# Sliding-window attention output: one bank copy, and the add of two halves moved into an accumulating DRAM transfer

## The chip, the cores and the metric

The kernel runs on one core of a Trainium2 chip. The metric is device time in microseconds, taken as the median of three runs. The profile records one execution.

The engines are named as the profile names them: PE is TensorE (its weight loads are PEld), DVE is VectorE, ACT is ScalarE, POOL is GpSimd, and SP is SyncE, which here only issues DMA transfers.

## The reference

One decoder layer over 2048 tokens with 16 meta tokens in front (model width 1024): RMSNorm, a combined input projection, two attention branches side by side (stick-breaking attention with 8 heads; sliding-window attention with 16 query heads, 2 key/value heads, a window of 128 and one sink logit per head), gates, two branch projections, a merge, an output projection, a residual and a final RMSNorm. The change lies in the sliding-window branch:

```python
def sliding_window_sink_attention(q, k, v, sinks, valid):
    ...
    scores = jnp.einsum('bnqhgd,bnkhd->bnhgqk', qb, kb) * scale      # per block of 128 queries, 256 keys
    scores = jnp.where(mask[None, :, None, None], scores, -jnp.inf)  # diff in [0, 128)
    probs = jax.nn.softmax(jnp.concatenate([scores, sink], axis=-1), axis=-1)[..., :-1]
    o = jnp.einsum('bnhgqk,bnkhd->bnqhgd', probs, vb)
    return o.reshape(B, L, Hq * d)

    y_sw = (o_sw * jax.nn.silu(sw_z)) @ w_branch_swa[l]
```

## The kernel before

Everything is float32. To keep its precision in matmuls, values are split into a high part (rounded) and a low part (the rest), and a product is made of three matmuls (high·high, high·low, low·high). Tokens are stored in reverse order, in four groups of 512 (`GT`), worked on as two halves, groups 2 and 3 first, then 0 and 1.

In each half come, in order: the projections of the sliding-window branch and part of the stick-breaking ones, the sliding-window attention (`window`), the stick-breaking attention (`stick`), and the gates. Projections run as `col_tile`: 24 matmuls of 128x512 into one of two banks `ps_g` (L412 to L414), then an evacuation by ACT and DVE. The attention is interleaved with projections by hand: `weave` takes one step of the main generator (projections) and then steps of the side generator (`attend`, later `stick`), paced by costs that each `yield` names. The order of PE's instructions is that program order. The order of the other engines' instructions, of the DMA issues on SP and of the DMAs on POOL included, is made by the framework's scheduler from its own cost model; waits are set by the framework from the data dependences.

`attend` runs 32 units per half: for each of four sets `s` of four heads (`kv = s // 2`), each of two groups `g`, and each of four blocks `i` of 128 queries. A unit passes through three steps:

- `scores`: 8 matmuls (L705) into the two banks `ps_z`, copied by ACT (L708) and masked by DVE (L709) into `sc`, whose sink column POOL fills (L698); row maximum (L711), exponentials with sums (L713), reciprocal (L714), scaling (L715).
- `turn`, three units later (`ULAG = 3`): four transposes (L739) into `ps_t`, then the split into `ph` (ACT, L114) and `pl` (DVE, L115), and four selects on POOL (L745) that build `pm`, in which the low part of one half of the keys and the high part of the other stand.
- `values`, a part of a unit later: six matmuls (L761) into the single bank `ps_o`. The left operand holds the high part of V in 64 columns and the low part in the other 64, so the bank's partitions 0 to 63 hold one partial output and 64 to 127 the other; their sum is the output of the block for four heads.

Before the change `values` copies the upper 64 partitions to a `tmp` tile (ACT, L763), and two DVE additions of 64x256 (L767) add them to the lower ones and lay the four heads out as two pairs of 128 rows in `os`, a tile with one buffer for four units. After the fourth unit two stores of 256 KB (through the helper `DMA`, L58, on SP's queue) go to the DRAM tiles `ow`.

`ow` is read again much later, by `gated`, after all the attention of its half. The tile pool of `window` is closed when its 32 units are through, and the pool of `stick` takes its memory; the first loads of `stick` are those of `kt`, `vc` and `q` (in `load_kv` and `load_q`), and its first matmul is L862. Between the last `values` and that matmul PE has gate projections.

The tile `tmp` is a ring of 9 buffers that many steps share; the weight splits on POOL are L110 and L111.

Of the kernel before, what the change touches and what calls it, by code (L numbers as in the profile page):

```python
# [7 lines left out]
F32 = mybir.dt.float32  # L8
# [3 lines left out]
ALU = mybir.AluOpType  # L12
# [4 lines left out]
P = 128  # L17
# [4 lines left out]
GT = 512  # L22
# [20 lines left out]
def f32(ap):  # L43
    return ap.bitcast(F32)
# [3 lines left out]
def tile_kernel(ctx, tc, x, xt, meta, metat, gain, w_in, w_sb, w_sw, w_out, sinks, fgain,  # L48
# [6 lines left out]
    V, A, G, T = nc.vector, nc.scalar, nc.gpsimd, nc.tensor  # L55

    def DMA(dst, src):
        nc.sync.dma_start(*(t.bitcast(F32) if t.dtype == F32R else t for t in (dst, src)))  # L58
# [6 lines left out]
    def ps(tag):  # L65
        return pp.tile([P, 512], F32, tag=tag, name="ps_" + tag, bufs={"g": 2, "z": 2, "zm": 1, "t": 2, "o": 1}[tag])
# [20 lines left out]
    def dram(name, shape, dt=F32):  # L87
        return dp.tile(shape, dt, tag=name, name=name)
# [9 lines left out]
    ow = [[dram(f"ow{p}_{g}", [P, GT]) for g in range(4)] for p in range(8)]  # L98
# [243 lines left out]
    def tmp(dt=F32, rows=P):  # L342
        return tp.tile([rows, GT], dt, tag="tmp", name="tmp", bufs=9)
# [259 lines left out]
    def window(half, groups, sp):  # L603
# [145 lines left out]
        def values(s, g, i, st):  # L749
            kv = s // 2  # L750
            blk = 4 * (g - groups[0]) + i
            if i == 0:
                os_[0] = sp.tile([P, 2, GT], F32, tag="os", name="os", bufs=1)
            o = ps("o")
            ph, pl, pm = st["p"]
            oc = o.rearrange("p (a q) -> p a q", a=4)
            for n in range(2):
                c = slice(HB * n, HB * n + HB)
                v = vv[:, blk + n, kv, :]
                for j, (lv, rp) in enumerate(((v, ph), (v, pl), (dv[kv, blk][:, n, :], pm))):  # L760
                    T.matmul(oc[:, :, c], lhsT=lv, rhs=rp[:, :, c], start=j == 0, stop=j == 2)  # L761
            t = tmp(rows=64)
            A.copy(t, o[64:128])  # L763
            ov = o[0:64].rearrange("p (b a q) -> p b a q", b=2, a=2)
            tv = t.rearrange("p (b a q) -> p b a q", b=2, a=2)
            for a in range(2):
                V.tensor_tensor(os_[0][64 * a:64 * a + 64, :, i * P:(i + 1) * P],  # L767
                                ov[:, :, a, :], tv[:, :, a, :], op=ALU.add)
            if i == 3:
                for pr in range(2):  # L770
                    DMA(ow[2 * s + pr][g], os_[0][:, pr, :])

        os_ = [None]
        ending = []

        def attend():
            units = [(s, g, i, {}) for s in range(4) for g in groups for i in range(4)]
            n = len(units)
            for u in range(n + ULAG):
                if u >= ULAG:  # L780
                    turn(*units[u - ULAG])
                yield 1.25
                if u < n:
                    last = 2 * units[u][0] + 1, units[u][1]
                    while last not in qs or (clock[0] < qs[last][1] and not ending):
                        yield 0
                    scores(*units[u])
                    if u < 4:
                        differences(0, 2 * u)
                    if u in (13, 15, 17, 19):  # L790
                        differences(1, u - 13)
                yield 0.9
                if u >= ULAG:
                    values(*units[u - ULAG])
# [150 lines left out]
    def put(hl, k, t):  # L945
        A.copy(hl[0][:, k, :], t)
        V.tensor_tensor(hl[1][:, k, :], t, f32(hl[0][:, k, :]), op=ALU.subtract)
# [307 lines left out]
    for half, groups in enumerate(halves):  # L1255
        gts = [lambda spec=spec: gate(*spec) for spec in specs[half]]
        with tc.tile_pool(name=f"swa{half}", bufs=1, side="left") as sp:
# [13 lines left out]
            q = [[lambda p=p: sw_q(p) for p in (2 * s, 2 * s + 1)] for s in range(4)]  # L1271
# [146 lines left out]
```

## Time and profile before

| | |
|---|---|
| median of three runs | 2132.24 us (2131.35 to 2132.43) |
| profiled execution: device time | 2134.33 us |
| profiled execution: span in the profile | 2132.6 us |
| granted TensorE clock | 0.999 |
| DMA | 390.93 MB, all issued from SP but for instruction fetches |

The profile's page lists busy time by engine, the span in 40 slices, the chain of work that ended last, and groups of instructions by source line, with their names as `output<-inputs`, their shapes, their count, and behind a bar the busy time in us and the mean of one in ns, then the idle time of that engine just before them and what ended it. Other views used below are: waits (who waited for whom: us in total, times, longest), busy time by stretch of time, the instructions of one tile or one line, and the order of time, where a row gives the start in us, the length in us, the engine, the line, the operation and its count; in brackets stands idle time before it and what ended it.

The two stretches in which `window` runs are 128 to 372 us and 870 to 1101 us; the first starts a little before with the last of the start-up.

### The profile page before, as it was taken

Reading aid. Unit: us, or ns where it says so; the run is one execution under the profiler, and the core shown is the slowest. Engines: PE = TensorE matmul, PEld = TensorE weight load, DVE = VectorE, ACT = ScalarE, POOL = GpSimd, SP = SyncE. Lnnn points to the kernel's source line nnn. Section 1 sums busy time; section 2 is a strip of 40 time slices with the busy share of each in tenths; the row PEclk is TensorE's granted clock in tenths of the full one; section 3 lists DMA queues with packets and bytes.
Section 4 is the critical chain, followed back from the end, with each engine's and each line's share of the span. In section 5 each row is a group of like instructions: output and inputs, shape, how many; then the busy total and the mean of one; then the engine's idle time right before and its main releaser. Section 6 shows DMA issues by size and latency. Waiting matters only on the chain.

```text
span 2132.6 us, 30750 instructions
## 1 busy us (share of the span) xinstructions
PE 2107.9 (99%) x10658; PEld 1751.0 (82%) x10658; DVE 1471.6 (69%) x2372; ACT 1078.4 (51%) x2461; POOL 268.9 (13%) x457
## 2 busy tenths in 40 slices
PE   8999999999999999999999999999999999999998
PEld 6788888888888888888888888888888888787886
DVE  7788986877877554887738888777773447454553
ACT  6677775555546335877735555555553213221121
POOL 2134343110000000232310000000000121000000
PEclk9999999999999999999999999999999999999999
DMA  9855554766448574434454334333324986568432
GB/s 336 293 186 191 177 187 170 236 193 195 147 170 321 207 256 153 160 128 175 145 178 157 122 117 139 109 118 103 116 89 170 359 288 212 177 216 308 149 94 89
DMA packets 170043, 390.93 MB, mean 183 GB/s; under 512 B 24448, under 2 KB 28288, under 8 KB 169888
## 3 DMA queue, kind: packets, MB, share of 16 engines
q1 hardware_dynamic: 169888, 388.97, 54.3%
q8 instruction: 84, 1.38, 0.3%
q14 instruction: 71, 0.58, 0.1%
HBM read 241.55 MB, written 145.18 MB: 181 GB/s over the span
## 4 chain that ended last, share of the span: by engine, by line
PE 85%; DVE 6%; ACT 3%; issue 2%; DMA 2%; POOL 0%; SPq 0%; ACTq 0%; DVEq 0%; POOLq 0%
PE ps_g L412 12%; PE ps_g L413 12%; PE ps_g L414 12%; PE ps_o L913 6%; PE ps_z L862 6%; PE ps_t L887 5%; PE ps_z L705 2%; PE ps_o L761 2%; PE ps_g L233 1%; PE ps_g L232 1%; PE ps_g L231 1%; PE ps_z L233 1%; PE ps_z L231 1%; PE ps_z L232 1%; PE ps_t L233 1%
## 5 line engine op out<-in xcount | busy, mean ns | idle before, releaser
L412 PE MATMUL ps_g<-xh,wh 128*128 128x512 f32 x1296 | 532.5, 411 | 7.6 <-ACT xh L1107 7.0
L414 PE MATMUL ps_g<-xh,wl 128*128 128x512 f32 x1296 | 509.3, 393 | 0.0
L413 PE MATMUL ps_g<-xl,wh 128*128 128x512 f32 x1296 | 509.2, 393 | 0.0
L876 DVE TENSOR_TENSOR_SCAN row<-row 128x512 f32<-128x512 f32 (+4 forms) x256 | 293.5, 1147 | 93.3 <-ACT row L866 40.4
L414 PEld LDWEIGHTS ps_g<-xh,wl 128*128 128x128 f32 x1296 | 243.8, 188 | 54.1
L412 PEld LDWEIGHTS ps_g<-xh,wh 128*128 128x128 f32 x1296 | 244.8, 189 | 47.2 <-ACT xh L1107 7.0
L866 ACT ACTIVATE row<-ps_z 128x512 f32<-128x512 f32 (+1 forms) x320 | 172.2, 538 | 212.4 <-PE ps_z L862 191.9
L413 PEld LDWEIGHTS ps_g<-xl,wh 128*128 128x128 f32 x1296 | 245.0, 189 | 38.1 <-DVE xl L1108 1.3
L114 ACT ACTIVATE wth<-ps_t 128x512 fp32r<-128x512 f32 (+1 forms) x320 | 170.7, 533 | 75.7 <-PE ps_t L887 73.8
L115 DVE SCALAR_TENSOR_TENSOR wtl<-ps_t,wth 128x512 fp32r<-128x512 f32 (+1 forms) x320 | 189.1, 591 | 25.6 <-ACT wth L114 25.1
L862 PE MATMUL ps_z<-kt,q 128*128 128x512 f32 (+3 forms) x640 | 185.5, 370 | 0.0
L887 PE MATMUL ps_t<-ident,row 128*128 128x128 f32 x1088 | 171.6, 273 | 0.1
L887 PEld LDWEIGHTS ps_t<-ident,row 128*128 128x128 f32 x1088 | 134.6, 140 | 33.7 <-DVE wtl L115 0.8
L862 PEld LDWEIGHTS ps_z<-kt,q 128*128 128x128 f32 x640 | 117.9, 188 | 23.9
L913 PE MATMUL ps_o<-wth,vc 128*128 128x512 f32 (+1 forms) x320 | 130.3, 407 | 0.8 <-ACT tmp L917 0.7
L913 PE MATMUL ps_o<-wtl,vc 128*128 128x512 f32 (+1 forms) x320 | 116.7, 365 | 0.0
L713 ACT ACTIVATE sc<-sc,nm 128x129 f32<-128x129 f32 x256 | 100.0, 393 | 27.9 <-DVE nm L711 26.6
L111 POOL TENSOR_TENSOR wl<-raw,wh 128x1024 fp32r<-128x1024 f32 (+1 forms) x28 | 59.9, 2138 | 325.8 <-ACT wh L108 297.0
L108 ACT CAST wh<-raw 128x1024 fp32r<-128x1024 f32 (+1 forms) x44 | 42.7, 971 | 89.2 <-PE ps_g L232 30.2
L874 DVE TENSOR_TENSOR_SCAN row<-row,mask 128x512 f32<-128x512 f32 (+2 forms) x64 | 67.9, 1066 | 19.9 <-ACT row L866 11.5
L567 ACT ACTIVATE tmp<-ps_g 128x512 f32<-128x512 f32 x84 | 50.2, 597 | 61.4 <-PE ps_g L414 49.9
L871 POOL TENSOR_SCALAR_AFFINE_SELECT row<-row 128x128 f32<-128x128 f32 x64 | 20.2, 315 | 469.5 <-ACT row L866 469.5
(435 smaller groups left out, 4092.0 us busy)
## 6 DMA issues: line engine op xcount, KB each, us to landing
wh<-h_in_w_in SPq DMA_DIRECT2D x66, 512.0 KB, 3.7
wl<-l_in_w_in SPq DMA_DIRECT2D x66, 512.0 KB, 4.6
raw<-in_w_in SPq DMA_DIRECT2D x50, 512.0 KB, 5.4
h_in_w_in<-wh SPq DMA_DIRECT2D x50, 512.0 KB, 3.4
l_in_w_in<-wl SPq DMA_DIRECT2D x50, 512.0 KB, 3.8
q<-qd SPq DMA_DIRECT2D x128, 128.0 KB, 3.2
vc<-vd SPq DMA_DIRECT2D x48, 256.0 KB, 2.9
kd<-tmp SPq DMA_DIRECT2D x32, 256.0 KB, 4.6
```

The costliest lines, as they stand in the source:

```text
L114: A.activation(h, acc, AF.Copy, scale=scale)
L115: V.scalar_tensor_tensor(l, acc, scale, f32(h), op0=ALU.mult, op1=ALU.subtract)
L412: T.matmul(acc, lhsT=wh[:, k, :], rhs=xh[g][:, k, :], start=k == 0, stop=False)
L413: T.matmul(acc, lhsT=wh[:, k, :], rhs=xl[g][:, k, :], start=False, stop=False)
L414: T.matmul(acc, lhsT=wl[:, k, :], rhs=xh[g][:, k, :], start=False, stop=k == KT - 1)
L713: A.activation(sc[:, hh, :], sc[:, hh, :], AF.Exp, bias=nm[:, hh:hh + 1], accum_out=den[:, hh:hh + 1])
L862: T.matmul(z[:, :w], lhsT=lq, rhs=kt[h][:, k0:k0 + w], start=t == 0, stop=t == 1)
L866: A.activation(r[:, :w], z[:, :w], AF.Sigmoid, scale=-1.0)
L874: V.tensor_tensor_scan(r[:, :w], r[:, :w], mask[:, :w], 1.0, op0=ALU.mult, op1=ALU.max)
L876: V.tensor_tensor_scan(r[:, :w], r[:, :w], r[:, :w], last[j] if n else 1.0, op0=ALU.mult, op1=ALU.min)
L887: T.transpose(tr[:, j * P:(j + 1) * P], rows_of[h, g, n - (j > i), j][:, k0:k0 + P], ident)
L913: T.matmul(o[:, :n], lhsT=v, rhs=r, start=first and r is wh, stop=last)
```

## The change

ACT copies the whole bank `ps_o` (both partial outputs, 128x512) into `os`, which now holds two units (128 partitions, four heads, 256 queries) with the same size and still one buffer. The `tmp` tile and the two DVE additions are gone. After every second unit the lower 64 partitions go by two plain stores to `ow`, and then the upper 64 partitions by two transfers issued from POOL with `accum_op=ALU.add`, which add to what stands in DRAM. Each of the four transfers moves 128 KB: 64 partitions, two heads, 256 queries. In place of 32 stores of 256 KB there are 64 plain ones and 64 accumulating ones. The accumulating transfers depend on the plain ones, since they read and write the same bytes.

```diff
         def values(s, g, i, st):
             kv = s // 2
             blk = 4 * (g - groups[0]) + i
-            if i == 0:
-                os_[0] = sp.tile([P, 2, GT], F32, tag="os", name="os", bufs=1)
+            if i % 2 == 0:
+                os_[0] = sp.tile([P, 4, 2 * P], F32, tag="os", name="os", bufs=1)
             o = ps("o")
...
-            t = tmp(rows=64)
-            A.copy(t, o[64:128])
-            ov = o[0:64].rearrange("p (b a q) -> p b a q", b=2, a=2)
-            tv = t.rearrange("p (b a q) -> p b a q", b=2, a=2)
-            for a in range(2):
-                V.tensor_tensor(os_[0][64 * a:64 * a + 64, :, i * P:(i + 1) * P],
-                                ov[:, :, a, :], tv[:, :, a, :], op=ALU.add)
-            if i == 3:
-                for pr in range(2):
-                    DMA(ow[2 * s + pr][g], os_[0][:, pr, :])
+            A.copy(os_[0][:, :, i % 2 * P:(i % 2 + 1) * P], oc)
+            if i % 2:
+                for n, put in ((0, DMA), (1, lambda o, i: G.dma_start(out=o, in_=i, accum_op=ALU.add))):
+                    for pr in range(2):
+                        put(ow[2 * s + pr][g][:, (i - 1) * P:(i + 1) * P].rearrange("(a d) t -> d a t", a=2),
+                            os_[0][64 * n:64 * n + 64, 2 * pr:2 * pr + 2, :])
```

## The prediction

> **What bounds the kernel now.** I read the page first, then busy time by stretch, TensorE's waits, the groups by line, and at last the order of time around the edited lines.
>
> ```profile
> span 2132.6 us, 30750 instructions
> PE 2107.9 (99%) x10658; PEld 1751.0 (82%) x10658; DVE 1471.6 (69%) x2372; ACT 1078.4 (51%) x2461; POOL 268.9 (13%) x457
> ```
>
> TensorE (PE) is busy nearly everywhere. An edit can win only the time in which PE stands idle near it, and loses all of what it makes PE wait. The edited function runs in two stretches, 128 to 372 us and 870 to 1101 us. This is the sum row of busy time over 128 to 250, 250 to 372, 870 to 985 and 985 to 1101 us, and below it PE's waits in the whole program that fall there:
>
> ```profile
> sum 475.00, PE 469.28 PEld 404.03 DVE 366.65 ACT 335.69 POOL 167.07; mean PE 117.32 PEld 101.01 DVE 91.66 ACT 83.92 POOL 41.77
> ```
>
> ```profile
> PE ps_zm L525 <- DVE tmp L115: 2.2, 2, 1.4
> PE ps_o L761 <- DVE os L767: 1.8, 2, 1.5
> PE ps_z L705 <- DVE sc L709: 1.2, 2, 0.7
> PE ps_o L761 <- POOL pm L745: 0.8, 2, 0.6
> ```
>
> (Columns: us in total, times, longest.) PE is idle for 475.00 − 469.28 = 5.7 us there: the whole prize. VectorE (DVE) ends most of it, the adds that the change removes (L767) 1.8 us.
>
> **What is removed.** The adds and their neighbours, from the groups by line:
>
> ```profile
> L767 DVE TENSOR_TENSOR os<-ps_o,tmp 64x256 f32<-64x256 f32 x128 | 52.9, 413 | 7.0 <-ACT tmp L763 5.7
> L917 ACT COPY tmp<-ps_o 128x512 f32<-128x512 f32 x32 | 18.8, 586 | 19.5 <-PE ps_o L913 18.4 <-DMA q<-qd 0.7
> L110 POOL TENSOR_SCALAR wh<-raw 128x1024 fp32r<-128x1024 f32 x21 | 25.5, 1215 | 75.0 <-DMA h_in_w_in<-wh 28.0 <-PE ps_t L423 18.2 <-PE ps_g L413 13.4
> L111 POOL TENSOR_TENSOR wl<-raw,wh 128x1024 fp32r<-128x1024 f32 (+1 forms) x28 | 59.9, 2138 | 325.8 <-ACT wh L108 297.0 <-DMA q<-qd 17.8 <-DMA raw<-in_w_sw 7.6
> ```
>
> 128 adds of 413 ns leave DVE: 52.9 us. Nearly all of it ran beside PE's matmuls, so only PE's idle time can come back: 0 to 5.7 us. I take 2.5: the 1.8 that waits on the adds by name, and a little of the 3.4 that waits on other DVE work. The bank `ps_o` also comes free about 0.8 us earlier, after the copy alone; the next unit's matmuls need it a whole unit later, so that is worth nothing more.
>
> **The copy.** ScalarE (ACT) copies the whole bank instead of half. In time by line:
>
> ```profile
> L763 ACT COPY tmp<-ps_o x32: 567/583/587, 129.6 to 366.5; 64x512 f32<-64x512 f32 x32
> L763 ACT COPY tmp<-ps_o x32: 569/583/586, 870.5 to 1098.0; 64x512 f32<-64x512 f32 x32
> ```
>
> The half-bank copy has a median of 583 ns, and the full-bank copy of L917 takes 586: 64 times 3 ns, nothing. The rows also give the rhythm: 31 gaps in 236.9 us is 7.64 us a unit in the first stretch, and 31 in 227.5 is 7.34 in the second.
>
> **The transfers.** Before, one pair of 256 KB stores for four units. After, for each two units two plain 128 KB stores on SyncE's queue (SP) and two accumulating ones on GpSimd's (POOL): 64 and 64.
>
> ```profile
> ow<-os SPq DMA_DIRECT2D x32, 256.0 KB, 2.3
> od<-tmp SPq DMA_DIRECT2D x64, 128.0 KB, 2.4
> tmp<-ow SPq DMA_DIRECT2D x16, 256.0 KB, 5.2
> L58 SPq DMA_DIRECT2D ow<-os x32: 319/403/772, 157.1 to 1099.9; - x32
> ```
>
> (The first three: KB each, median us to landing.) SP gets 32 more issues of 0.403 us, 13 us over 475, in which it mostly waits for inputs anyway: nothing. The halved transfer lands no sooner: 128 KB from 64 partitions (`od`) 2.4 us, 256 KB from 128 partitions 2.3. The Trainium skill, page "DMA: Bandwidth & Descriptors", section "Rules for kernel authors", says that two transfers to disjoint partition halves gain nothing over one of 128 partitions, and speaks against the new cut; the two rows agree.
>
> Now a chain exists that did not before. The accumulating store reads and rewrites what the plain one wrote, so POOL waits until that one has landed, and `os` (one buffer, now refilled every two units instead of four) comes free only when both accumulating stores have landed. From the start of the odd unit's copy: copy 0.59, first plain store landed 2.3 later, at 2.9. Two POOL issues: the trace has no DMA from POOL, so an issue costs between SP's 0.4 and POOL's longest common instruction (L111, 2.14); I take 1.2, as L110, a plain POOL instruction. That is 5.3. Landing: at least a store's 2.3, at most a read-back and a store one after the other, 5.2 + 2.3 = 7.5; I take 3.0, nearer the store, since one transfer does both. **Round trip 8.3 us**, bounds 2.9 + 0.8 + 2.3 = 6.0 and 2.9 + 4.3 + 7.5 = 14.7. The Trainium skill, same page, section "Anatomy of one DMA", fits a POOL-issued DMA with 2.0 us plus bytes over 436 GB/s, an estimate of 2.3 us here; by that alone the round trip would be 7.6 and the sum about 6 us instead of 11. No run shows such a transfer yet.
>
> **Who waits.** Three queues get a new wait at their head.
>
> ACT: the next even unit's copy waits for `os`; behind it stand `ph` (the first step to the next values), the exponentials and the evacuations of `ps_g`. The round trip exceeds the mean gap of 7.64 or 7.34 us by 0.7 to 1.0 us, 30 times: 25 us of later copies. ACT has 475.00 − 335.69 = 139 us idle, 4.4 a pair, and PE feels it only where the path copy, `ph`, `pl`, `pm`, values has no cover. Two units of that path, one tight and one loose:
>
> ```profile
> 257.68 0.58 ACT L763 COPY tmp<-ps_o 64x512 f32<-64x512 f32 x1
> 260.58 1.80 POOL L745 TENSOR_SCALAR_AFFINE_SELECT pm<-pl 64x256 fp32r<-64x256 f32 x2 [0.73 <-DVE pl L115]
> 262.48 0.28 PE L761 MATMUL ps_o<-pm,xs 128*128 128x256 f32 x1
> ...
> 241.16 0.58 ACT L763 COPY tmp<-ps_o 64x512 f32<-64x512 f32 x1
> 243.44 0.89 POOL L745 TENSOR_SCALAR_AFFINE_SELECT pm<-pl 64x256 fp32r<-64x256 f32 x2 [0.81 <-DVE pl L115]
> 247.06 0.28 PE L761 MATMUL ps_o<-pm,xs 128*128 128x256 f32 x1
> ```
>
> In the first the select ends at 262.38 and its matmul starts at 262.48: cover 0.1 us. In the second it is 2.7. I take one sixth of the 25 us: **+4**, bounds 0 and 25.
>
> POOL: while it waits for the plain store and then issues for 2.4 us, the selects of `pm`, the sink columns of `sc` and some weight copies (L110, L111) stand behind. By the rows above, the second pair of selects starts 2.28 and 2.90 us after a copy starts, and the plain store lands at 2.9. Mostly the selects are just ahead; where they are not, they start 2.4 us late against cover of 0.1 to 2.7, about 1 us for PE. I take five pairs of 32: **+5**, bounds 0 and 32 × 2.3 = 74.
>
> SP: a later copy makes its store later, with weight loads behind it; ACT's row covers that already.
>
> The handover to the next stage is the third place. Its tiles take this pool's memory, and the first K loads wait for the last `ow` store. Waits of SP's queue at the two handovers, and both in order of time:
>
> ```profile
> SPq L58 <- DMA ow<-os: 1.9, 1, 1.9
> SPq L58 <- DMA ow<-os: 4.0, 1, 4.0
> ```
>
> ```profile
> 366.50 0.58 ACT L763 COPY tmp<-ps_o 64x512 f32<-64x512 f32 x1 [2.15 <-PE ps_o L761]
> 367.99 0.80 SPq L58 DMA_DIRECT2D ow<-os  x2
> 370.82 0.50 SPq L58 DMA_DIRECT2D kt<-kd  x1
> 374.68 2.37 SPq L58 DMA_DIRECT2D q<-qd  x4
> 381.28 0.39 PE L862 MATMUL ps_z<-kt,q 128*128 128x512 f32 x1
> ...
> 1098.01 0.58 ACT L763 COPY tmp<-ps_o 64x512 f32<-64x512 f32 x1
> 1099.50 0.86 SPq L58 DMA_DIRECT2D ow<-os  x2
> 1104.55 1.12 SPq L58 DMA_DIRECT2D kt<-kd  x2
> 1112.45 1.89 SPq L58 DMA_DIRECT2D q<-qd  x3
> 1120.30 0.63 PE L862 MATMUL ps_z<-kt,q 128*128 128x512 f32 x2
> ```
>
> ```profile
> DMA to landing us min/median/max: 2.7/3.9/4.7
> DMA to landing us min/median/max: 3.7/3.8/4.4
> ```
>
> (The last two: `q` loads at each handover.) First handover: copy ends 367.1, plain store landed 369.4, two issues 371.8, landed 374.8, against K loads at 370.82: 4.0 us later. The last `q` load that PE needs was issued about 376.5 and landed 3.9 later at 380.4; PE wanted it at 381.28: cover 0.9, so PE stands 3.1. Second: 1098.6, landed after issue and the 4.0 of that place about 1103.0, 1105.4, 1108.4, against 1104.55: 3.9 later; `q` came at 1113.7 + 3.8 = 1117.5 for 1120.30, cover 2.8, PE stands 1.1. Together **+4.2**, bounds 0.8 (issue 0.4, landing 2.3) and 17 (2.14, 7.5).
>
> **Sum.** −2.5 + 4 + 5 + 4.2 = +10.7 us. The profiled execution took 2134.33 us, 1.7 more than its span and 2.1 more than the median of 2132.24; it would take 2145, and the median goes to **2143 us**. A measurement of this kernel can tell about 0.2%, 4.3 us, from no change; the forecast is slower by 0.5%.
>
> **Rivals.** *DVE was the brake* (0.13). DVE is busy 366.65 of 475 us, and three of the four waits quoted end at DVE or at POOL behind it. If the round trip stays below the gaps, about 7 us, and POOL's issues fall behind the selects, all 5.7 us of idle time can go and the handovers cost 0.8: −4.9, 2127.3. Against it: it needs landing near a plain store's, and issues near SP's 0.4.
>
> *A wash* (0.22). Round trip between 6 and 8 us, so that ACT's copy waits a little where ACT would idle, POOL costs nothing, the handovers 2 to 4: −2.5 + 3 = about 0, 2133. For it: 139 us of idle ACT, and DVE's relief shortens `pl`, which feeds the selects.
>
> *The accumulating write is slow* (0.17). It fetches its destination from DRAM before it writes; at the bound of 7.5 us the round trip is 2.9 + 2.4 + 7.5 = 12.8. That passes the mean gap of 7.5 by 5.3 and ACT's idle time of 4.4 a pair by 0.9: 32 × 0.9 = 29 for PE, handovers 7.6 + 5.5 = 13, POOL 5, less 2.5: +45, 2177. It decides once the round trip passes about 12 us.
>
> That the add doesn't take place I exclude: the low half is in the output only by this transfer.
>
> **How the numbers follow.** The forecast (+4.3 to +30 us) has 0.48, the slow write 0.17, both slower: 0.65. The wash is "same", 0.22; the relief "faster", 0.13. The range runs from 2128 (nearly all of PE's idle time regained) to 2180 (the slow write). The forecast's own range is 2137 to 2162.
>
> **What would show it.** Right: no L767; DVE down by about 53 us; DMAs on POOL whose issue takes about 1.2 us; ACT's copy waiting for an `ow` transfer; K loads at both handovers some 4 us later relative to the last copy, with PE idle before L862; PE idle between 128 and 372 us up, ended by POOL `pm` or ACT. Wrong: PE's idle sum in these stretches at or below 5.7 us, and L862 without a wait: then the round trip was hidden. If PE's idle time grows at places that wait for weights, the new stores held up SP, which I put at nothing.

## The result, and the profile after

| | before | after |
|---|---|---|
| median | 2132.34 us | 2165.82 us (2160.09 to 2168.11) |
| ratio to before, 95% interval | | 1.0151 [1.0139, 1.0163] |
| span of the profiled execution | 2132.6 us | 2165.1 us |
| granted TensorE clock | 0.999 | 0.995 |

Slower by 33.5 us; the forecast was 10.7. The sign and most of the places were right, the size was not. The page of the kernel after, its lines of the span and of busy time by engine:

```profile
span 2165.1 us, 30797 instructions
...
PE 2120.7 (98%) x10658; PEld 1757.1 (81%) x10658; DVE 1424.1 (66%) x2244; ACT 1069.4 (49%) x2461; POOL 318.6 (15%) x521
```

The tile `os` after, its rows by line (durations in ns min/median/max) and its transfers on SP's queue (KB each, median us to landing):

```profile
L762 ACT COPY os<-ps_o x64: 562/587/607, 128.8 to 1129.7; 128x512 f32<-128x512 f32 x64
L58 SPq DMA_DIRECT2D ow<-os x64: 586/599/897, 140.8 to 1131.6; - x64
L764 POOL DMA_DIRECT2D ow<-os x64: 948/977/1323, 143.6 to 1135.4; - x64
...
DMA to landing us min/median/max: 2.4/4.3/8.1
```

```profile
ow<-os SPq DMA_DIRECT2D x64, 128.0 KB, 2.5
```

The copy takes 587 ns as forecast, an issue on POOL 0.98 us for the 1.2 assumed. DVE is relieved of 47.5 us (the forecast had 53) and of 128 instructions, and in the time nothing of it is seen. PE is busy 12.8 us *longer* with the same 10658 matmuls: some of them ran slower.

Where the time went is seen from milestones that both traces have, the starts of the first and the last `values` matmul on `ph` (L761) of each half and the first matmul of `stick` (L862 before, L858 after):

| stretch, us | before | after | difference |
|---|---|---|---|
| first attention stretch | 128.7 to 365.9 | 127.9 to 380.8 | +15.7 |
| first handover | 15.4 | 18.8 | +3.4 |
| to the second half's first values | 486.0 | 486.9 | +0.9 |
| second attention stretch | 867.3 to 1097.5 | 886.5 to 1129.2 | +12.5 |
| second handover | 22.8 | 23.8 | +1.0 |
| the rest, to the end | 1012.3 | 1012.1 | −0.2 |

So 28.2 of the 32.5 us in the spans lie in the two attention stretches, for which the forecast had 6.5. Busy time in these stretches (sum rows; the windows are cut at the milestones), first before, then after:

```profile
sum 467.60, PE 461.88 PEld 398.04 DVE 361.29 ACT 334.51 POOL 165.76; mean PE 115.47 PEld 99.51 DVE 90.32 ACT 83.63 POOL 41.44
```

```profile
sum 495.80, PE 473.45 PEld 403.29 DVE 314.28 ACT 325.04 POOL 211.46; mean PE 118.36 PEld 100.82 DVE 78.57 ACT 81.26 POOL 52.86
```

PE's idle time grows from 5.7 to 22.4 us, and its busy time by 11.6 us for the same work. The waits after (us in total, times, longest):

```profile
PE ps_o L761 <- ACT os L762: 8.8, 4, 4.4
...
PE ps_o L761 <- POOL pm L745: 6.5, 10, 2.1
PE ps_z L858 <- DMA gs<-tmp: 3.3, 1, 3.3
...
POOL ow L764 <- DMA ow<-os: 39.3, 25, 8.4
ACT os L762 <- DMA ow<-os: 31.6, 13, 5.1
ACT os L762 <- issue: 26.4, 10, 4.9
```

(The wait for `gs` is the first handover's.) ACT's copy (L762) waits 31.6 us for the accumulating stores by name, and 26.4 us more are put down to "issue", right ahead of copies in the same position. In the trace 26 of the 30 even units' copies start within 0.3 us of the landing of the last accumulating store. PE waits for that copy and for the selects, seldom, but up to 4.4 us at a time. The longest such wait, in order of time, cut to the lines that matter:

```profile
350.82 0.57 ACT L762 COPY os<-ps_o 128x512 f32<-128x512 f32 x1
...
351.42 1.24 SPq L58 DMA_DIRECT2D ow<-os  x2
...
354.31 0.98 POOL L764 DMA_DIRECT2D ow<-os  x1 [0.53 <-DMA ow<-os]
...
355.36 2.39 POOL L111 TENSOR_TENSOR wl<-raw,wh 128x1024 fp32r<-128x1024 f32 x1
...
355.73 0.60 PE L739 MATMUL ps_t<-ident,sc 128*128 128x128 f32 x4
...
357.70 0.98 POOL L764 DMA_DIRECT2D ow<-os  x1
...
364.85 0.59 ACT L762 COPY os<-ps_o 128x512 f32<-128x512 f32 x1 [5.11 <-DMA ow<-os]
...
365.49 0.39 PE L761 MATMUL ps_o<-ph,vv 128*128 128x256 f32 x1 [4.39 <-ACT os L762]
...
366.34 1.05 PE L739 MATMUL ps_t<-ident,sc 128*128 128x128 f32 x4
...
368.14 0.87 POOL L745 TENSOR_SCALAR_AFFINE_SELECT pm<-ph 64x256 fp32r<-64x256 f32 x2 [7.58 <-ACT ph L114]
```

Read it downwards. The odd unit is copied at 350.82. The first accumulating store is issued 3.5 us later, the second only at 357.70, because a weight split (L111) stands between the two on POOL. It lands 6.1 us after the end of its issue, and only then does the next copy start: a round trip of 14.0 us. By then PE has run out of other work and stands for 4.39 us, since the single bank `ps_o` has to be copied before it can be written again. And the stop is not over when PE starts: four transposes take 1.05 us right after it, against 0.60 just before (L739). The granted clock (the figure behind the instruction count) shows the same in windows of 8 us around another stop, one of 3.24 us that ends at 185.03:

```profile
176.00:184.00 8.00, 5.79 (x30) 1.00 0.83 195
184.00:192.00 8.00, 6.97 (x44) 0.79 0.44 134
```

Five such windows of the two stretches stand below 1.00: three at 0.79, and the two around the stop shown above at 0.89 and 0.90. Narrower windows show what lies behind the 0.79, half the clock for 3.4 us and then the full one:

```profile
185.30:188.70 3.40, 3.40 (x26) 0.51 0.21 77
188.70:192.00 3.30, 3.30 (x21) 0.99 0.63 161
```

The five windows together are 8 × (3 × 0.21 + 0.11 + 0.10) = 6.7 us of lost matmul time, more than half of PE's longer busy time; the rest of it I can't assign. The Trainium skill, page "TensorE: Matmul & The Clock Gate", Part 1, says that the clock falls to half after an idle window of about 3.4 us. The trace agrees in kind, though not in the length of the stop: the stops of 3.24 and 4.39 us were followed by a lower clock, and so were two of 1.94 and 2.15 us, each with a shorter one some microseconds before it; one of 1.88 us was not.

### The profile page after: what moved, and what is told of

The parts are those of the page before. It is cut to its first block, busy times and chain, and to the rows that moved or that the text cites. A ratio compares the mean times of both kernels' runs of the same rounds, so it can differ in the third digit from the quotient of the medians.

```text
span 2165.1 us, 30797 instructions
## 1 busy us (share of the span) xinstructions
PE 2120.7 (98%) x10658; PEld 1757.1 (81%) x10658; DVE 1424.1 (66%) x2244; ACT 1069.4 (49%) x2461; POOL 318.6 (15%) x521
## 4 chain that ended last, share of the span: by engine, by line
PE 69%; DMA 4%; ACT 3%; DVE 3%; issue 2%; POOL 1%; SPq 0%; ACTq 0%; POOLq 0%; DVEq 0%
PE ps_g L412 8%; PE ps_g L413 7%; PE ps_g L414 7%; PE ps_o L909 6%; PE ps_z L858 6%; PE ps_t L883 5%; DMA ow<-os 3%; PE ps_g L233 1%; PE ps_g L232 1%; PE ps_z L233 1%; PE ps_z L232 1%; PE ps_z L231 1%; PE ps_g L231 1%; PE ps_t L233 1%; PE ps_t L232 1%
## 5 line engine op out<-in xcount | busy, mean ns | idle before, releaser
L862 ACT ACTIVATE row<-ps_z 128x512 f32<-128x512 f32 (+1 forms) x320 | 172.4, 539 | 218.7 <-PE ps_z L858 194.3
L858 PE MATMUL ps_z<-kt,q 128*128 128x512 f32 (+3 forms) x640 | 186.4, 371 | 4.7 <-DMA gs<-tmp 3.3
L858 PEld LDWEIGHTS ps_z<-kt,q 128*128 128x128 f32 x640 | 118.3, 189 | 29.5 <-issue 4.5
L111 POOL TENSOR_TENSOR wl<-raw,wh 128x1024 fp32r<-128x1024 f32 (+1 forms) x28 | 61.2, 2187 | 317.8 <-ACT wh L108 278.3
L745 POOL TENSOR_SCALAR_AFFINE_SELECT pm<-ph 64x256 fp32r<-64x256 f32 x128 | 60.9, 476 | 134.8 <-ACT ph L114 130.7
```

The source lines that it names most:

```text
L858: T.matmul(z[:, :w], lhsT=lq, rhs=kt[h][:, k0:k0 + w], start=t == 0, stop=t == 1)
L862: A.activation(r[:, :w], z[:, :w], AF.Sigmoid, scale=-1.0)
```

## The experiments

The theory: `os` is held for the whole round trip of the accumulating store, and where the trip outlasts what PE has in hand, PE stops (and its clock falls). Rivals: POOL's hold (the selects stand behind its wait for the plain store); the accumulating writes' traffic in itself; the transfers' number; and the handover.

Two measures serve all runs: the sum of the two attention stretches, and the round trip, from the start of an odd unit's copy to the start of the next even unit's copy, pair by pair from the order of time (30 pairs). Stretches, handovers and trips are read from one profiled execution of each kernel. The times of before in the same sessions were 2132.74 to 2133.79.

| kernel | time, us | ratio, 95% interval | stretches, us | handovers, us |
|---|---|---|---|---|
| before | 2132.34 | | 467.4 | 15.4, 22.8 |
| after | 2165.82 | 1.0151 [1.0139, 1.0163] | 495.6 | 18.8, 23.8 |
| e1, `tmp` ring of 8 | 2166.02 | 1.0156 [1.0141, 1.0171] | 493.9 | 17.8, 23.7 |
| e2, two `os` buffers | 2136.60 | 1.0013 [1.0004, 1.0023] | 464.1 | 16.9, 22.8 |
| e3, add at the later load | 2156.40 | 1.0107 [1.0092, 1.0122] | 462.3 | 15.3, 22.8 |
| e4, plain, nothing to wait for | 2129.35 | 0.9985 [0.9975, 0.9994] | 463.9 | 15.3, 22.8 |
| e5, plain, same wait | 2135.23 | 1.0011 [1.0002, 1.0021] | 468.0 | 15.4, 22.8 |
| e6, buffers of one unit | 2141.41 | 1.0037 [1.0024, 1.0051] | 472.0 | 16.9, 22.8 |
| e7, last pair on DVE | 2159.39 | 1.0128 [1.0112, 1.0143] | 493.4 | 15.3, 22.8 |
| e8, add from DRAM to DRAM | 2130.08 | 0.9987 [0.9978, 0.9997] | 462.2 | 16.1, 22.8 |
| e9, one joint transfer | 2162.30 | 1.0138 [1.0124, 1.0152] | 489.7 | 17.1, 23.2 |
| e10, e2 and e7 together | 2130.88 | 0.9989 [0.9980, 0.9998] | 464.0 | 15.3, 22.8 |
| e11, e8 again | 2130.09 | 0.9988 [0.9979, 0.9997] | 462.3 | 16.5, 22.8 |
| e12, plain, long trip | 2179.64 | 1.0215 [1.0198, 1.0232] | 501.3 | 20.7, 23.3 |

**e1 and e2: room for a second `os`.** A second buffer needs the memory of one `tmp` buffer, so e1 takes that buffer away alone, and e2 uses it.

```diff
-        return tp.tile([rows, GT], dt, tag="tmp", name="tmp", bufs=9)
+        return tp.tile([rows, GT], dt, tag="tmp", name="tmp", bufs=8)
...
-                os_[0] = sp.tile([P, 4, 2 * P], F32, tag="os", name="os", bufs=1)
+                os_[0] = sp.tile([P, 4, 2 * P], F32, tag="os", name="os", bufs=2)   # e2 only
```

> A control for the next run: the changed kernel with 8 instead of 9 buffers of the shared ring tmp, which frees the 2 KB that a second os buffer needs. Round-trip theory (the changed kernel loses its time because the one os buffer is held until the accumulating stores have landed, so that ACT's next copy, and PE behind it, wait) and POOL theory (it loses its time because POOL, in order, stands at the accumulating stores and the selects for pm come late) both expect the time of the changed kernel, 2166 us, within 5 us; the change dropped one tmp tile per unit, so the ring has slack.

> As the control, with two os buffers. Nothing on POOL is removed. Round-trip theory: a copy now waits for the stores of the pair before the last, about 22 us earlier against a round trip of 8 to 15 us, so the ACT waits for os go from about 32 us to under 5, the stops of PE of 3 us and more vanish, and of the 33 us some 25 come back: 2137 to 2143 us, the handovers' 4.5 us staying. POOL theory: the selects are as late as before, 2160 us or more.

The smaller ring changes nothing. The second buffer gives back 29.4 us, nearly all of the loss, with every accumulating store still there. Waits of e2 that answer to those of the kernel after:

```profile
POOL ow L764 <- DMA ow<-os: 43.1, 26, 8.5
ACT os L762 <- PE ps_o L761: 16.9, 17, 2.2
...
PE ps_o L761 <- POOL pm L745: 1.1, 2, 0.8
```

```profile
sum 464.30, PE 461.48 PEld 398.13 DVE 315.33 ACT 326.75 POOL 211.73; mean PE 115.37 PEld 99.53 DVE 78.83 ACT 81.69 POOL 52.93
```

POOL still waits 43.1 us for the plain stores, more than in the kernel after, and the selects cost PE 1.1 us: POOL's hold is not the cause. The copies wait for no transfer any more. PE's idle time in the stretches is 2.8 us, half of before, so DVE's relief is there once the new wait is gone. (The profiled execution of e2 took 2133.34 us, the fastest of its ten, with a median of 2136.60.)

**e3: the add moved to the reader.** Both halves go to DRAM plainly from SP; `gated` loads both and adds them on DVE.

```diff
-    ow = [[dram(f"ow{p}_{g}", [P, GT]) for g in range(4)] for p in range(8)]
+    ow = [[dram(f"ow{p}_{g}", [2, P, GT]) for g in range(4)] for p in range(8)]
...
-        if src is od:
+        if src is od or src is ow:
...
```

> No accumulating transfer: the low half goes by a plain store from SP to a DRAM tile of its own, and is added where the gating step loads it, as the other branch does already. Both theories: the two attention stretches lose nothing (first to last values as before the change, within 2 us), the handovers are as before or 1 us earlier; at the end 32 more loads of 256 KB and 32 DVE adds of 0.7 to 0.9 us (about 25 us of DVE work) come in, beside a busy PE. Expected 2128 to 2138 us. If the time stays above 2150, neither theory holds and the doubled stores themselves or the full-bank copy cost it.

The attention stretches are among the shortest, 462.3 us, and the handover as before; yet the kernel takes 2156.4. The loss is elsewhere: from the last score matmul to the end it takes 549.2 us against 523.1 before. These waits are new there:

```profile
PE ps_g L412 <- ACT tmp L567: 6.6, 2, 5.2
PE ps_g L231 <- ACT tmp L567: 4.5, 1, 4.5
PE ps_g L231 <- ACT ringl L207: 3.4, 3, 1.7
```

PE is idle for 16.8 us there, before for 0.3, and the granted clock is 0.98 and 0.97 in the first two thirds of that part. So the expected time was missed for a reason of this experiment, not of the change: the adds went from a stretch where DVE has cover to one at the end that has less. That it is the adds rather than the doubled loads is not shown; the waits name ACT. By stretches the run speaks for the theory.

**e4 and e5: plain writes with and without the wait.** Both replace the accumulating write by a plain one of the same size from POOL. In e4 it goes to a DRAM tile of its own, so that it waits for nothing; the low part is left out of the output. In e5 it overwrites the plain store at the same place, and so waits as in the kernel after; here the high part is left out.

```diff
-                for n, put in ((0, DMA), (1, lambda o, i: G.dma_start(out=o, in_=i, accum_op=ALU.add))):
+                for n, put in ((0, DMA), (1, lambda o, i: G.dma_start(out=o, in_=i))):
...
-                        put(ow[2 * s + pr][g][:, (i - 1) * P:(i + 1) * P].rearrange("(a d) t -> d a t", a=2),
+                        put(ow[2 * s + pr][g][n][:, (i - 1) * P:(i + 1) * P].rearrange("(a d) t -> d a t", a=2),   # e4 only
...
```

> The POOL transfers stay, at the same places and sizes, but write plainly to a DRAM tile of their own: nothing is accumulated and they don't wait for the plain store; the low half is left out of the output. Round-trip theory: the trip shrinks to copy 0.6, two issues of 1.0 and one landing of 2.4 to 4.5 us, together 5 to 7, below the gap of 7.3 to 7.6: 2135 to 2145 us. POOL theory in the form that the issues cost (64 of 1 us): 2155 us or more, since they remain; in the form that the wait for the plain store's landing costs: as the round-trip theory, so this run alone does not tell that form apart, the run with two os buffers does.

> The changed kernel with the POOL transfers at the same places, on the same bytes and with the same wait for the plain store, but writing plainly: the low half replaces the high one instead of being added. Only the accumulation is gone. A plain POOL store landed 1.2 us sooner than an accumulating one in the earlier runs (3.3 against 4.5 us). If the loss is the whole chain (plain store, its landing, two POOL issues, second landing) on one buffer, shortening it by 1.2 us gives back a part: 2148 to 2160 us. If the accumulation itself is what makes it too long, nearly all comes back: below 2142 us. If the chain's length doesn't matter, 2166.

Without the wait the stretches are 3.5 us shorter than before the change. With the wait but no accumulation the kernel loses 4.1 us of that again, not 32. What e5 changes in the trip, in the transfers' row (KB each, median us to landing), after and e5:

```profile
ow<-os POOLq DMA_DIRECT2D x64, 128.0 KB, 4.5
```

```profile
ow<-os POOLq DMA_DIRECT2D x64, 128.0 KB, 3.6
```

The landing, counted from the start of the issue, is 0.9 us shorter; of these 0.4 are the issue itself, which takes POOL 0.61 instead of 0.98 us. The mean round trip falls from 10.49 to 9.45 us, and trips over 11 us from 12 of 30 to 4. One microsecond less in the mean saves 27.6 us in the stretches. That is either a threshold, or accumulation costs something that the trip does not show; e9 and e12 were made to tell these apart. (e2, which has every accumulating store and loses nothing in the stretches, already speaks against the second.)

**e6: smaller buffers in the same memory.** Two `os` buffers of one unit each, stored unit by unit, with twice as many transfers of half the size.

```diff
-            if i % 2 == 0:
-                os_[0] = sp.tile([P, 4, 2 * P], F32, tag="os", name="os", bufs=1)
+            os_[0] = sp.tile([P, 4, P], F32, tag="os", name="os", bufs=2)
...
```

> The same 4 KB of os cut into two buffers of one unit each, every unit storing its own 64 KB pieces: twice as many transfers, 128 plain and 128 accumulating ones, with 512-byte rows. Round-trip theory: a copy waits for the stores of the unit before the last, 15 us earlier, against a trip of 8 to 15 us, so most waits go: 2136 to 2150 us although POOL issues 63 us more. POOL theory: with twice the issues and waits at POOL it is slower than the changed kernel, 2175 us or more.

256 transfers instead of 128 with the same bytes accumulated, and the stretches need 23.6 us less than after: the number of transfers is not it either, and one unit of cover is enough, as no copy waits for a transfer here. But with twice the issues POOL's hold is not free:

```profile
PE ps_o L760 <- POOL pm L745: 6.3, 6, 2.0
```

At the longest of these six waits POOL waits 0.70 us for a plain store and issues for 0.99 us between two pairs of selects. The stretches are 7.9 us longer than those of e2.

**e7: the last pair as before.** Of the last group of each half, units 2 and 3 are added on DVE and stored plainly.

```diff
+            end = (s, g) == (3, groups[1]) and i > 1
...
+            if end:
+                t = tmp(rows=64)
+                A.copy(t, o[64:128])
...
+                    V.tensor_tensor(os_[0][64 * a:64 * a + 64, :, cs], ov[:, :, a, :], tv[:, :, a, :], op=ALU.add)
```

> The changed kernel, but the last pair of units of each half adds on DVE and stores once, as before the change. Only the two handovers are touched: the first K loads no longer wait for an accumulating store. The handovers cost 3.5 and 1.0 us in the traces (last values to first score matmul: 15.4 to 18.8 and 22.8 to 23.8), so 4.5 us less than the changed kernel: 2159 to 2163 us. If the time stays at 2166, the handover's cost was covered by something else.

The handovers are 15.3 and 22.8, as before the change; the stretches stay long. **e10** joins it with e2:

> Two os buffers (one tmp buffer fewer makes room), and only the last pair of units of each half is added on DVE as in the kernel before, so neither the round trip nor the handover has an accumulating write in its path. If round trip and handover are the whole loss, 2130 to 2134 us and the first score matmul of the next stage 15 to 16 us after the last values matmul in the first half, as before; if the POOL hold or the transfers cost time by themselves, 2138 or more.

Stretches and handovers are then at or under their lengths before, and the time is 2130.88, 34.9 us less than after. Round trip and handover together are the whole loss.

**e8 and e11: the accumulation taken off the buffer's path.** Both halves are stored plainly from SP, the low one to a DRAM tile of its own, and `os` is free when those have landed. Two units later POOL adds tile to tile in DRAM, 32 transfers of 256 KB.

```diff
+    owl = [[dram(f"owl{p}_{g}", [P, GT + P]) for g in range(4)] for p in range(8)]
...
-                for n, put in ((0, DMA), (1, lambda o, i: G.dma_start(out=o, in_=i, accum_op=ALU.add))):
+                for n, to in ((0, ow), (1, owl)):
...
+                while adds:
+                    adds.pop(0)()
+                if i == 3:
+                    adds.extend(lambda k=2 * s + pr, g=g: G.dma_start(out=ow[k][g], in_=owl[k][g][:, :GT], accum_op=ALU.add)
+                                for pr in range(2))
...
```

> A version that computes the same: both halves are stored plainly from SP (the low one to a DRAM tile of its own), and POOL adds the low tile to the high one from DRAM to DRAM two units later, 32 transfers of 256 KB. No SBUF buffer waits for the accumulation. Round-trip theory: the attention stretches as with the plain stores (234 and 228 us against 237 and 230 before), the handovers as before, nothing added at the end: 2126 to 2132 us, level with or slightly faster than the kernel before. POOL theory: 32 waits on POOL remain; over 2140 us.

> The kernel of e8_dramadd once more, in five rounds, for a narrower interval: both halves go out plainly from SP, and POOL adds the low DRAM tile to the high one two units later. 2128 to 2132 us, ratio 0.997 to 0.9995 if its gain over the kernel before is real; 1.000 to 1.002 if the first result was chance.

Transfers and waits of e8:

```profile
ow<-owl POOLq DMA_DIRECT2D x32, 256.0 KB, 5.6
```

```profile
ACT os L763 <- PE ps_o L762: 13.2, 12, 2.2
ACT os L763 <- DMA owl<-os: 2.9, 2, 1.6
```

The accumulating transfer, of twice the size, now takes 5.6 us, longer than in the kernel after, and no copy waits for it: the copies wait 2.9 us for transfers instead of 31.6. The output is that of the kernel before, and the time is below it in both sessions, 0.9987 [0.9978, 0.9997] and 0.9988 [0.9979, 0.9997]: 2.7 us, of the 5.1 to 5.2 us by which the attention stretches are shorter; the first handover is some 1 us longer, and the rest is not assigned.

**e9: one POOL issue instead of two.** A joint DRAM tile for both pairs lets one plain and one accumulating transfer of 256 KB serve two units.

```diff
...
-                    for pr in range(2):
-                        put(ow[2 * s + pr][g][:, (i - 1) * P:(i + 1) * P].rearrange("(a d) t -> d a t", a=2),
-                            os_[0][64 * n:64 * n + 64, 2 * pr:2 * pr + 2, :])
+                    put(owj[s][g][:, :, (i - 1) * P:(i + 1) * P].rearrange("r (a d) t -> d (r a) t", a=2),
+                        os_[0][64 * n:64 * n + 64])
```

> One plain and one accumulating transfer of 256 KB for each two units, into a DRAM tile that holds both pairs; os as in the kernel after, every low half still added by an accumulating write. POOL issues once instead of twice, so the last landing should come about 2 us sooner: round trip from 10.1 to 10.9 us down to 8 to 9. Theory (the length of the round trip against what TensorE tolerates, near 9.5 us): the attention stretches are regained for the most part, 2133 to 2142 us. Rival (accumulating writes cost time by themselves, by their traffic or their slow DMA queue, whatever waits for them): the same bytes are accumulated, 2158 us or more.

The time fell where the rival had put it, and my step to it failed first: the trip is 9.93 us, not 8 to 9. The larger plain store lands in 3.6 us instead of 2.5, so POOL issues at a median of 4.5 us after the copy instead of 3.55, and the accumulating one still lands late. Rows of e9 (`os` tile: issue on POOL; then all its transfers, min/median/max to landing):

```profile
L765 POOL DMA_DIRECT2D ow<-os x32: 1002/1016/1195, 145.4 to 1128.8; - x32
...
DMA to landing us min/median/max: 3.1/4.3/8.0
```

8 of 30 trips are over 11 us, between e5's 4 and after's 12. By the mean alone, 9.93 against 9.45 in e5, 22 us more in the stretches is hard to explain; by the long trips it is in order, but so is it for the rival. What the copies wait for by name, first in e9 and then in e5, goes with the stretches better than the mean trip does:

```profile
ACT os L763 <- DMA ow<-os: 44.3, 20, 6.7
```

```profile
ACT os L762 <- DMA ow<-os: 18.4, 11, 3.2
```

That accumulation adds something of its own e9 can't exclude.

**e12: a long trip without accumulation.** e5 with one small plain transfer more, of 16 KB of the same data, which must wait for the one before it; the high part is left out of the output as in e5.

```diff
...
+                put(ow[2 * s + 1][g][:, (i - 1) * P:(i + 1) * P].rearrange("(a d) t -> d a t", a=2)[0:8],
+                    os_[0][64:72, 2:4, :])
```

> The kernel of e5_overwrite (no accumulating write anywhere), with one small transfer more on POOL behind each set: 16 KB of the same high half written once more over the same bytes, which has to wait until the transfer before it has landed, and so keeps os about 3 us longer. It tells a long round trip from accumulation. If TensorE loses by round trips over some 11 us whatever makes them long, the mean trip rises from 9.5 to about 12 and the attention stretches lose 30 us or more: 2165 to 2185 us with a later handover. If the accumulating write by itself costs the time (its traffic, its queue), 2135 to 2142.

2179.64 us: no accumulating write anywhere, and a larger loss than with them. The mean trip is 12.23 us, 20 of 30 are over 11, and PE waits where the theory says:

```profile
PE ps_o L761 <- ACT os L762: 24.9, 13, 4.9
```

POOL waits 84.1 us for transfers of `ow` there, twice as long as after, but the selects cost PE only 2.1 us. Five kernels with one `os` buffer and the wait, by their trips:

| | e5 | e9 | e1 | after | e12 |
|---|---|---|---|---|---|
| mean trip, us | 9.45 | 9.93 | 10.46 | 10.49 | 12.23 |
| trips over 11 us, of 30 | 4 | 8 | 10 | 12 | 20 |
| PE idle at trips over 11 us, us | 1.3 | 8.8 | 14.2 | 15.4 | 27.3 |
| PE idle at the other trips, us | 2.5 | 6.7 | 7.6 | 5.8 | 0.5 |
| stretches less those of e2, us | 3.9 | 25.6 | 29.8 | 31.5 | 37.2 |

(PE idle: its idle time from one odd unit's copy to the next one's, added up over the 30 pairs.) That a long trip alone is enough for such a loss is shown. The loss is steep between mean trips of 9.5 and 10 us and much flatter beyond. In all but e5 most of PE's idle time lies at trips over 11 us, yet 11 us is no threshold: of the 12 such trips of the kernel after, 6 go with at most 0.3 us, and one of 9.8 us goes with 1.5. So the trip's length alone doesn't say whether PE stops; that the rest is the work PE has in hand at that place is a reading, and why e5 and e9 lie so far apart stays open.

## Why the prediction was right in its sign and wrong in its size

- **DVE's relief, −2.5**: about right. The six kernels whose copies wait little or not at all for a transfer (e2, e3, e4, e8, e10, e11) have stretches 3.3 to 5.2 us shorter than before.
- **Copy, SP's extra issues, 0**: right. e4 has all of them and is faster than before.
- **The round trip, 8.3 us**: too short; 10.49 in the mean, and 8.2 to 14.0 pair by pair. In the mean of the 30 pairs the first accumulating issue starts 3.84 us after the copy's start instead of 2.9, and the second 1.37 us after the first instead of 1.2 (in 12 of all 32 pairs selects or a weight split, L110 or L111, stand between them). The second issue takes 1.12 us instead of 1.2, its landing comes 3.94 us after its end instead of 3.0, and the next copy starts 0.22 us after that. So the late first issue and the landing are errors of 0.9 us each. The landing is well inside the bounds that I gave (2.3 to 7.5), but I took a value next to the plain store. (The 4.5 us of the transfers' row count from the start of the issue; the 2.3 us that the prediction sets beside my value is further off.)
- **ACT's later copy, +4**: this is the mis-sized term. Measured it is 29.8 us (e1 less e2), above even the bound of 25. Two steps of it failed. The excess of the trip over the mean gap is 3.0 us a pair, not 0.7 to 1.0, because the trip was set too short; 30 times 3.0 is 90 us, and a sixth of that would have been 15. And PE loses a third of the 90 us, not the sixth that I took: PE's stops gather at the long trips (15.4 of its 21.2 us of idle time in the 30 pairs lie at the 12 trips over 11 us), which a mean does not show, and behind the longest stops the matmuls run slower as well. Of the 28.2 us in the stretches 16.6 are idle time, and 11.6 are matmuls that took longer, 6.7 of them by the clock.
- **POOL's hold, +5**: wrong, about 0 in this kernel. POOL waits just as long in e2, and there the selects cost PE 1.1 us. Only with twice the issues, in e6, do they cost 6.3.
- **Handovers, +3.1 and +1.1**: right in sum, +3.4 and +1.0, and e7 removes both. The size of the delay was not right. At the first one:

```profile
381.36 0.59 ACT L762 COPY os<-ps_o 128x512 f32<-128x512 f32 x1 [2.15 <-PE ps_o L761]
381.98 1.24 SPq L58 DMA_DIRECT2D ow<-os  x2
384.91 1.97 POOL L764 DMA_DIRECT2D ow<-os  x2 [7.13 <-DMA ow<-os]
393.11 1.13 SPq L58 DMA_DIRECT2D kt<-kd  x2
...
399.60 0.47 PE L858 MATMUL ps_z<-kt,q 128*128 128x512 f32 x1 [3.31 <-DMA gs<-tmp]
```

  The K loads start 11.2 us after the copy's end, against 3.7 before: 7.4 later, not 4.0; in the trace the last landing comes 6.0 us after its issue's end instead of 3.0. PE's cover was larger than I had worked out by some 3 us, so the two errors cancel, and that the sum fits is luck.
- **The rivals**: the slow accumulating write was the closest, in mechanism more than in its numbers: it wanted a landing of 7.5 us and a trip past 12, and the loss began near 10. The relief of DVE (2127) is what e8 comes near to. The wash was wrong by the trip, which it put at 6 to 8 us.

## What to carry to other kernels

When a transfer takes over work from an engine, cost the time for which it holds its source buffer, from the copy to the last landing and pair by pair, not the work that the engine saves: one more buffer, or a store whose landing nobody waits for, decided 29 to 36 us here, the engine's 50 us of adds 3 to 5. Against the mean rhythm a trip may look short enough; here nearly three quarters of TensorE's idle time lay at the trips over 11 us, 12 of 30. And a stop can cost more than its length: the one of 3.2 us was followed by 3.4 us of matmuls at half the clock.

If an accumulating write is wanted, let it read from DRAM behind plain stores, so that it lies on no buffer's path.

## What the runs showed of the hardware

- Counted from the start of the issue, an accumulating transfer of 128 KB from 64 partitions lands in 4.5 us (median, kernel after), a plain one from the same queue in 3.6 at the same place (e5) and 3.3 where it waits for nothing (e4). One from SP lands in 2.4 to 2.5 us, in e4 in 3.5; of these few landings are in the traces. The accumulating issue takes POOL 0.98 us, a plain one 0.61.
- The landing varies far more than the issue: 3.0 to 8.1 us over the accumulating transfers of the kernel after, and 2.3 to 7.0 over the plain ones from POOL in e5.
- After a PE stop of 3.2 us the granted clock was 0.51 for 3.4 us and then 0.99. After one of 4.4 us four transposes took 1.05 us instead of 0.60.
